# A transformer layer with two attention branches: the forgetting gates are issued behind the first branch, one weight split is held behind the keys, and the row sums of the modulation change places

## The chip, the cores and the metric

The kernel runs on one core of a Trainium2 chip. The metric is device time in microseconds (us) of one execution; lower is better. Three runs of the kernel before the change took 765.37, 765.66 and 765.74 us; the median is 765.66.

## The reference

One decoder layer on 512 positions of width 1024, in float32. Six modulation rows come from a conditioning vector, two attention branches read one projection, and a gated MLP with a short convolution follows.

```python
mod = c @ w_ada + b_ada
sh1, sc1, gt1, sh2, sc2, gt2 = split(mod, 6)
u = x * (1 + sc1) + sh1
q_a, k_a, v_a, f_a, q_b, k_b, v_b, g_a, g_b = split(u @ w_in)
log_f = log_sigmoid(f_a + b_forget)          # 8 heads
cum = cumsum(log_f)
# A, forgetting attention: softmax(q k^T / 8 + cum[t] - cum[s]), s <= t
# B, stick-breaking: A[t,s] = beta[t,s] * prod_{s<j<t}(1 - beta[t,j]),
#    beta = sigmoid(q k^T / 8), s < t
merged = sigmoid(g_a) * (y_fox @ w_fox_proj) + sigmoid(g_b) * (y_sb @ w_sb_proj)
x = layer_norm(alpha * x + (1 + gt1) * (merged @ w_o))
u2 = x * (1 + sc2) + sh2
h_gate, h_val = split(causal_depthwise_conv(u2 @ w_up, width 3))
x = layer_norm(alpha * x + (1 + gt2) * ((silu(h_gate) * h_val) @ w_down))
```

Each branch has 8 heads of 64; the MLP is 2816 wide.

## The kernel before

**Products in three matmuls.** A float32 operand is kept as two tiles of a reduced format: a high part, which ACT makes by a copy (`hi_of`, L99), and a low part, which DVE makes by subtracting the high part from the operand (`lo_of`, L102). A product is three matmuls of 128x128 weights on 512 columns: high by high, high by low, low by high (`mm3`, L131 to L133).

**Items.** Weights come in 128x1024 tiles, *items*, in one list. An item is a DMA on the queue of SyncE (SP) into one of four raw buffers (`LOADS`), and a procedure: the split of weights (`split_proc` and `cut_proc`: high wh, low wl; for the v weights `v_proc`: wvh, wvl; for w_o `wo_proc`: woh, wol), or a *row sum* (`ada_proc`, `mod_col`): modulation values that are first needed after the attention are computed by DVE as a product of a tile of w_ada with the broadcast conditioning row, summed over the columns (L200, 128x1024), and the bias is added (L203). `weights(i, ahead)` issues loads up to item i+3 and runs the procedures up to item i+ahead; a load that needs a raw buffer first runs the procedure that frees it. So an item's place in the list decides when its DVE work is issued, and which loads stand behind it.

**The stream.** The projections (`proj`, `vproj`), branch projections (`bproj`) and the first part of w_o (`o_part`, L714 to L718) are generators in one list, `stream`. `fill(n)` issues n steps of matmuls from it, between the steps of attention, so that PE has work while a head's scores pass through ACT and DVE. `add_pair`, `add_wv`, `add_gate`, `add_ada` and `add_bproj` (L643 to L680) build stream and items together; `add_ada` adds row sums.

**Heads.** The stick-breaking branch (`br` 1) comes first, in pairs of heads, then the forgetting one. For each head `stage_a` makes scores (`scores`, L469 and L470: with s1 and m1, and with s2 and m2, whose last four rows hold the cumulated gates or their counterparts), the sigmoids on ACT (L477: om, one minus beta; L478: pt, beta), and for each of three blocks a reverse running product on DVE (`scan`, L489) and the product with beta (L490). Two one-element memsets on POOL go with it: om's (L486, block 2 only) ahead of the scan, and pt's (L491) behind the product. `stage_b` transposes the weights on PE through the bank set (`turn`, L532) and splits them (ph, pl, and ptc0 and ptc1 for the last blocks). `stage_c` multiplies by v, and adds the two halves into yf on DVE (L567).

**First heads.** Heads 0 and 1 are written out (from L767), with `chain` on: every operation on PE, ACT and DVE is then pinned behind the one issued before it on its engine. In the trace, operations that pass through it have the line of the helper (L68). Elsewhere a scheduler orders the instructions by the code's order and by estimated times. POOL and the DMAs are not pinned.

**Attention tiles.** When the early pool is closed, `open_att` opens a pool in its space: ptc, the s2 and m2 tiles. Memsets on POOL set the rows that hold the gates' counterparts (L325, L328, L330, L331). `fpad`, the padded weights of the forget logits, is one of the tiles in the space that is given up. Its last matmul is in `first_mm(KT - 1, (2, 7))`, group 7; group 2 is the query of pair 1.

**Gates.** `forget_evac` (L336) copies the two halves of the forget logits from their PSUM bank (fq, two copies on ACT), behind the first two heads. `forget` (L340) is issued at head 5: it is pinned behind the last sigmoid of the head before: an add on DVE, then Abs, Exp and Ln on ACT, a DVE operation and the running sum on DVE, and the split into `chi`. `decay_rows` copies the rows of chi by POOL's DMA queue into the s2 and m2 tiles of a forgetting head, once that head's tiles are free.

## Time and profile before

| | |
|---|---|
| median of 3 runs | 765.66 us (765.37 to 765.74) |
| the profiled execution | 764.82 us |
| its span in the trace | 763.0 us |
| granted TensorE clock, mean | 0.995 |
| PE busy | 746.4 us, 98% |
| DVE busy | 550.8 us, 72% |
| ACT busy | 351.9 us, 46% |
| POOL busy | 118.3 us, 16% |
| memory traffic, mean | 129 GB/s |

The engines are PE (matmuls), DVE and ACT (elementwise), POOL and SP, which issues the loads. A row of the timeline gives the start in us from the span's start, the time in us, the engine, line, operation, output and inputs, and in brackets the idle time of the engine ahead of it and what ended that. A row of the waits gives an engine's operation, the one that it waited for, and the total, the count and the longest in us. A row of the windows gives for each engine its busy time with the number of instructions, in the order PE, weight load, DVE, ACT, POOL, SP, and then the granted clock, the DMA share and the rate. Matmuls overlap their neighbours, so their pace is read from their starts. In a row of the DMA issues the last number is the median time from issue to landing.

### The profile page before, as it was taken

What the parts mean: (1) busy time and instruction counts of PE and PEld (TensorE: products, weight loads), DVE (VectorE), ACT (ScalarE), POOL (GpSimd) and SP (SyncE); (2) the same over time, 40 slices, a digit from 0 to 9 for tenths busy, and PEclk for the clock granted to TensorE, in tenths of its full rate; (3) what the DMA queues carried; (4) which work ended last, traced back from release to release, by engine and by line L of the source; (5) the groups of instructions that cost most, each with busy time, mean ns of one, the idle gap of its engine ahead of it and who ended that gap; (6) DMA issues with size and microseconds to landing.
All of it is one profiled execution on the core that took longest, in us unless ns stands there. A gap on an engine that the chain in (4) does not pass through costs nothing.

```text
span 763.0 us, 9469 instructions
## 1 busy us (share of the span) xinstructions
PE 746.4 (98%) x3494; PEld 620.8 (81%) x3494; DVE 550.8 (72%) x893; ACT 351.9 (46%) x586; POOL 118.3 (16%) x130
## 2 busy tenths in 40 slices
PE   8999999899999999999999999999999999999995
PEld 5878788788888888877889888888888888888885
DVE  6977898847787986387897787666666675444866
ACT  3366769537666664242256334444444433122300
POOL 2011000200010000000000950000000134945400
PEclk9999999999999999999999999999999999999998
DMA  8941332313432435545424334343343214423202
GB/s 319 405 161 55 112 111 82 113 37 130 159 119 83 152 128 164 188 141 188 177 62 155 142 126 129 132 139 111 114 134 111 82 56 167 137 84 111 82 34 77
DMA packets 30881, 99.41 MB, mean 130 GB/s; under 512 B 4178, under 2 KB 4690, under 8 KB 30835
## 3 DMA queue, kind: packets, MB, share of 16 engines
q1 hardware_dynamic: 29970, 97.69, 37.7%
q0 software_dynamic: 864, 1.12, 0.5%
q8 instruction: 27, 0.44, 0.3%
q14 instruction: 20, 0.16, 0.1%
HBM read 96.63 MB, written 2.11 MB: 129 GB/s over the span
## 4 chain that ended last, share of the span: by engine, by line
PE 82%; ACT 7%; DVE 6%; DMA 3%; issue 2%; POOL 0%; DVEq 0%; ACTq 0%
PE ps L131 15%; PE ps L132 15%; PE ps L133 15%; PE ps L1006 5%; PE ps L1007 5%; PE ps L1008 5%; PE ps L283 5%; PE ps L560 2%; DMA raw<-in_wa 2%; PE ps L532 2%; ACT wh L99 2%; PE ps L717 1%; PE ps L718 1%; PE ps L716 1%; DVE wl L102 1%
## 5 line engine op out<-in xcount | busy, mean ns | idle before, releaser
L102 DVE TENSOR_TENSOR wl<-raw,wh 128x1024 fp32r<-128x1024 f32 (+2 forms) x101 | 139.9, 1386 | 104.3 <-ACT wh L99 104.0
L99 ACT ACTIVATE wh<-raw 128x1024 fp32r<-128x1024 f32 (+2 forms) x101 | 104.8, 1041 | 112.5 <-PE ps L1008 38.3
L131 PE MATMUL ps<-u2h,wh 128*128 128x512 f32 (+1 forms) x376 | 141.4, 376 | 0.0
L133 PE MATMUL ps<-u2h,wl 128*128 128x512 f32 (+1 forms) x376 | 141.2, 376 | 0.0
L132 PE MATMUL ps<-u2l,wh 128*128 128x512 f32 (+1 forms) x376 | 141.2, 375 | 0.0
L131 PE MATMUL ps<-uh,wh 128*128 128x512 f32 x213 | 84.2, 395 | 1.3 <-ACT fq L68 1.3
L132 PE MATMUL ps<-ul,wh 128*128 128x512 f32 x213 | 83.4, 392 | 0.0
L133 PE MATMUL ps<-uh,wl 128*128 128x512 f32 x213 | 83.1, 390 | 0.0
L131 PEld LDWEIGHTS ps<-u2h,wh 128*128 128x128 f32 x376 | 70.7, 188 | 12.9
L133 PEld LDWEIGHTS ps<-u2h,wl 128*128 128x128 f32 x376 | 70.7, 188 | 12.7
L132 PEld LDWEIGHTS ps<-u2l,wh 128*128 128x128 f32 x376 | 70.7, 188 | 12.7
L627 POOL TENSOR_TENSOR raw<-raw,gt 128x1024 f32<-128x1024 f32 x22 | 60.7, 2766 | 79.2 <-DMA raw<-in_wdn 75.8
L1006 PE MATMUL ps<-wh,hh 128*128 128x512 f32 x128 | 49.8, 389 | 0.0
L1007 PE MATMUL ps<-wl,hh 128*128 128x512 f32 x128 | 49.8, 389 | 0.0
L1008 PE MATMUL ps<-wh,hl 128*128 128x512 f32 x128 | 49.8, 389 | 0.0
L200 DVE SCALAR_TENSOR_TENSOR raw<-raw,cbc 128x1024 f32<-128x1024 f32 x32 | 39.1, 1222 | 14.4 <-DMA raw<-in_wa 14.2
L131 PEld LDWEIGHTS ps<-uh,wh 128*128 128x128 f32 x213 | 40.0, 188 | 9.8 <-ACT fq L68 1.7
L133 PEld LDWEIGHTS ps<-uh,wl 128*128 128x128 f32 x213 | 40.0, 188 | 8.7
L132 PEld LDWEIGHTS ps<-ul,wh 128*128 128x128 f32 x213 | 40.1, 188 | 7.7
L99 ACT ACTIVATE hh<-cv 128x512 fp32r<-128x512 f32 x22 | 13.9, 632 | 61.6 <-DVE cv L986 61.6
L985 ACT ACTIVATE cv<-cv 128x512 f32<-128x512 f32 x22 | 13.9, 632 | 52.3 <-DVE cv L980 52.2
L979 DVE SCALAR_TENSOR_TENSOR cv<-ps,cw,cv 128x511 f32<-128x511 f32 x44 | 32.7, 743 | 2.5 <-ACT cv L978 2.5
(221 smaller groups left out, 1424.3 us busy)
## 6 DMA issues: line engine op xcount, KB each, us to landing
raw<-in_wup SPq DMA_DIRECT2D x44, 512.0 KB, 3.3
raw<-in_wa SPq DMA_DIRECT2D x32, 512.0 KB, 3.3
raw<-in_wct SPq DMA_DIRECT2D x29, 512.0 KB, 3.3
raw<-in_wdn SPq DMA_DIRECT2D x22, 512.0 KB, 3.1
wa<-in_wa SPq DMA_DIRECT2D x14, 512.0 KB, 7.5
raw<-in_wp SPq DMA_DIRECT2D x8, 512.0 KB, 4.1
raw<-in_wo SPq DMA_DIRECT2D x8, 512.0 KB, 3.8
raw<-in_w SPq DMA_DIRECT2D x7, 452.0 KB, 8.1
```

The source lines that it names most:

```text
L99: S.activation(o, i, AF.Copy, scale=scale)
L102: return V.tensor_tensor(o, i, fl(hi), ALU.subtract)
L131: PE.matmul(ps, wh, ah, start=first, stop=False)
L132: PE.matmul(ps, wh, al, start=False, stop=False)
L133: PE.matmul(ps, wl, ah, start=False, stop=last)
L200: V.scalar_tensor_tensor(wt[:, c], wt[:, c], 1.0, cbc[:, c], ALU.mult, ALU.mult, accum_out=raw[:, e : e + 1])
L283: PE.matmul(grp[g], w, u, start=j == 0 and n == 0, stop=j == KT - 1 and n == (1 if g == 7 else 2))
L627: G.tensor_tensor(r, r, gt[1], ALU.mult)
L979: V.scalar_tensor_tensor(t[:, 1:], ps[:, 0:511], cw[:, n, 1:2], t[:, 1:], ALU.mult, ALU.add)
L1006: PE.matmul(ps, hh[j][:, tb], w[0], start=first, stop=False)
L1007: PE.matmul(ps, hh[j][:, tb], w[1], start=False, stop=False)
L1008: PE.matmul(ps, hl[j][:, tb], w[0], start=False, stop=last)
```

## The change

- **The gates.** `forget_evac` is issued right behind `stage_b` of head 0, ahead of the query of pair 1, so under `chain`. `forget` moves from the head of n = 5 to n = 6, ahead of `stage_a` of the first forgetting head, pinned behind head 7's last sigmoid. The rows of all four first forgetting heads are then copied at once, since the stick-breaking heads whose tiles they take have been scored.
- **First heads.** The three matmuls of group 2 for the last k go ahead of the first scores; those on fpad stay behind them.
- **The hold.** For the projections of k, of pairs 2 and later, `proj` first asks for one split less, and issues that one behind the second copy of the pair's second key (`m1`), by `issue_after`.
- **Items.** The 24 row sums stood in the list as 8 with the pairs 5 and 6 (two behind each of q and k), 8 with the gates of the second branch and 8 with its branch projections. Now 3 stand with pair 3, 3 with the last three gates of the first branch, 3 with the queries of pairs 5, 6 and 7, 4 with the first branch's projections, 8 with the second branch's gates as before, and 3 with its branch projections. The v weights come behind q, not k, of a pair, and one more behind pair 3's gates. `vproj` asks for its splits further on by one tile for each block of rows from the third.

```diff
@@ -96,7 +96,7 @@
         return ap.bitcast(F32)
 
     def hi_of(o, i, scale=1.0):
-        S.activation(o, i, AF.Copy, scale=scale)
+        return S.activation(o, i, AF.Copy, scale=scale)
 
     def lo_of(o, i, hi):
         return V.tensor_tensor(o, i, fl(hi), ALU.subtract)
@@ -392,7 +392,7 @@
         r = slice(64 * hh, 64 * hh + 64)
         m1 = z(F32R, "m1")
         hi_of(m1[0:64, :], ps[r, :])
-        hi_of(m1[64:128, :], ps[r, :])
+        state["m"] = hi_of(m1[64:128, :], ps[r, :])
         n = slot_free(idx(br, h))
         m2 = m2z[h] if br == 1 and h < 2 else m2t[n]
         lo_of(m2[0:64, :], ps[r, :], m1[0:64, :])
@@ -436,7 +436,7 @@
 
     def vproj(j, last):
         ps = bank()
-        weights(last, 0)
+        weights(last + max(0, j - 1), 0)
         tb = slice(j * P, (j + 1) * P)
         for k in range(KT):
             h, l = wvs[k]
@@ -449,13 +449,16 @@
 
     ahead = [0]
 
-    def proj(n, after):
+    def proj(n, after, hold=False):
         ps = bank()
-        h, l = weights(n, ahead[0])
+        h, l = weights(n, ahead[0] - hold)
         for k in range(KT):
             mm3(ps, col(h, k), col(l, k), uh[k], ul[k], k == 0, k == KT - 1)
             yield 3
         after(ps)
+        if hold:
+            with tc.issue_after(state["m"].ins):
+                weights(n, ahead[0])
 
     ROWS = ((2,), (3,), (1, 0))
 
@@ -649,9 +652,9 @@
     marks = {}
     seq = PAIRS
 
-    def add_proj(n, after):
+    def add_proj(n, after, hold=False):
         proc = cut_proc if 0 < len(items) <= CUT else split_proc
-        stream.append((proj, (add_item(wct[TILES.index(n)], proc), after)))
+        stream.append((proj, (add_item(wct[TILES.index(n)], proc), after, hold)))
 
     wpi = {}
 
@@ -664,10 +667,11 @@
         br, pr = seq[p]
         for c, ev in (("q", q_evac), ("k", k_evac)):
             if (c, p) in TILES:
-                add_proj((c, p), lambda ps, ev=ev: ev(br, pr, ps))
+                add_proj((c, p), lambda ps, ev=ev: ev(br, pr, ps), p > 1 and c == "k")
                 marks[(p, c)] = len(stream)
-                add_ada({5: 2, 6: 2}.get(p, 0))
-                add_wv(p)
+                if c == "q":
+                    add_ada(p > 4)
+                    add_wv(p)
 
     wvi = []
 
@@ -677,7 +681,7 @@
 
     def add_gate(br, j):
         add_proj(("sb" if br == 1 else "fox", j), gate_after(br, j))
-        add_ada(1 - br)
+        add_ada(br == 0 or j > 4)
 
     gb = list(range(KT))
     for p, ng in ((1, 1), (2, 2), (3, 2), (4, 3)):
@@ -688,6 +692,9 @@
         for _ in range(ng):
             add_gate(1, gb.pop(0))
             add_wv(p)
+        if p == 3:
+            add_wv(p)
+            add_ada(3)
     marks["y1"] = len(stream)
     bj = list(range(KT))
     for p in (5, 6, 7):
@@ -696,6 +703,7 @@
             if bj:
                 j = bj.pop(0)
                 add_bproj(1, j, lambda m, j=j: ma.__setitem__(j, m))
+                add_ada(j % 2)
 
     mh, ml = [], []
 
@@ -732,7 +740,8 @@
     for j in range(3, KT):
         add_gate(0, j)
     for j in range(KT):
-        add_ada()
+        if j % 2 == 0:
+            add_ada()
         add_bproj(0, j, merge(j))
         if j:
             wos.append(add_item(wo[j - 1], wo_proc))
@@ -769,8 +778,9 @@
     for hh in range(2):
         q_half(1, 0, grp[0], hh)
         k_half(1, 0, grp[1], hh)
+    first_mm(KT - 1, (2,))
     scores(1, 0, 2)
-    first_mm(KT - 1, (2, 7))
+    first_mm(KT - 1, (7,))
     st0.close()
     open_att()
     sigmoids(0, 2)
@@ -802,6 +812,7 @@
         turn(1, 0, e)
     process()
     stage_b(1, 0)
+    forget_evac()
     q_half(1, 1, grp[2], 0)
     q_half(1, 1, grp[2], 1)
     fill(24)
@@ -814,21 +825,18 @@
         v_evac(1, j, 0, vf[j])
     process()
     process()
-    forget_evac()
     ahead[0] = AHEAD
     chain["on"] = False
     heads = [(br, 2 * p + e) for br, p in seq for e in range(2)]
-    last = hd[heads[1]]['last']
     for n, (b, h) in enumerate(heads):
-        if n == 5:
-            forget(last)
         f1, f2, f3 = FILL[n // 8]
         if n + 2 < 16:
             if n % 2 == 0:
                 fill_to(marks[(n // 2 + 1, "k")])
                 fill(LEAD)
                 f1 -= LEAD
-            last = hd[heads[n + 1]].get("last")
+            if n == 6:
+                forget(hd[heads[n + 1]]["last"])
             stage_a(*heads[n + 2])
         fill(f1)
         if n + 1 < 16:
```

POOL's queue at the first heads. First before, from the first scan's memset on (om is head 0's block 2, m_n and s_n the m2 and s2 tiles; the words behind a row are the semaphores it waits for):

```order
L486 MEMSET om_571 128x1 [waits Activation_49,Pool_49]
L491 MEMSET pt_572 128x1 [waits Activation_49]
L325 MEMSET m_2_552 4x512 [waits DVE_49,Pool_49]
L325 MEMSET m_3_553 4x512
L325 MEMSET m_0_550 4x512 [waits DVE_49]
L325 MEMSET m_1_551 4x512
L328 MEMSET ptc_542 128x128 [waits DMAHW0_49,PE_49,Pool_49]
L328 MEMSET ptc_543 128x128
L328 MEMSET ptc_544 128x128 [waits DVE_49,PE_49]
L328 MEMSET ptc_545 128x128
```

The same memsets after the change, the rows up to the first scan's:

```order
L328 MEMSET ptc_544 128x128 [waits DVE_49,PE_49,Activation_49]
L328 MEMSET ptc_545 128x128
L330 MEMSET s_0_546 4x512 [waits Pool_49]
L330 MEMSET s_1_547 4x512
L331 MEMSET s_0_546 2x512 [waits Pool_49]
L331 MEMSET s_1_547 2x512 [waits Pool_49]
L330 MEMSET s_2_548 4x512
L330 MEMSET s_3_549 4x512
L331 MEMSET s_2_548 2x512 [waits Pool_49]
L331 MEMSET s_3_549 2x512 [waits Pool_49]
L489 MEMSET om_571 128x1 [waits Activation_49,Pool_49]
L494 MEMSET pt_572 128x1 [waits Activation_49]
```

The two memsets of head 0's scan stood ahead of the twenty of the attention tiles and stand behind them now. (Lines from L460 on are three higher after the change.)

ACT's order around the gates. Before, in the work of heads 4 and 5 (om and pt are sigmoids, m key copies, wvh splits of the v weights, fq the gates):

```order
L477 ACTIVATE om_1225<-ps_1207 128x512
L478 ACTIVATE pt_1226<-ps_1207 128x512
L99 ACTIVATE m_244_1232<-ps_1145 64x512 x2
L343 ACTIVATE fq_498<-fq_499 8x512
L344 ACT_TABLE_LOAD
L344 ACTIVATE fq_498<-fq_498 8x512
L99 ACTIVATE m_245_1236<-ps_1145 64x512 x2
L99 ACTIVATE wvh_1245<-raw_1148 128x512
L99 ACTIVATE ptc_542<-ps_1289 128x384
L99 ACTIVATE wvh_1249<-raw_1148 128x512
L345 ACT_TABLE_LOAD
L345 ACTIVATE fq_498<-fq_498 8x512
```

After, behind head 7's last sigmoids (vv are v's splits, ph the high parts of the turned weights):

```order
L480 ACTIVATE om_1520<-ps_1502 128x512
L481 ACTIVATE pt_1521<-ps_1502 128x512
L99 ACTIVATE vv_1533<-ps_1462 128x2x2x64
L99 ACTIVATE ptc_542<-ps_1570 128x384
L343 ACTIVATE fq_498<-fq_499 8x512
L99 ACTIVATE vv_1536<-ps_1462 128x2x2x64
L99 ACTIVATE ph_1558<-ps_1553 128x512
L344 ACT_TABLE_LOAD
L344 ACTIVATE fq_498<-fq_498 8x512
L99 ACTIVATE ph_1566<-ps_1562 128x384
L345 ACT_TABLE_LOAD
L345 ACTIVATE fq_498<-fq_498 8x512
```

The four operations and their table loads have left the stretch before the turning of head 3's and 4's weights, and stand between the splits behind the stick-breaking branch's end.

DVE's order where the first part of w_o starts. Before (wol low parts of w_o, sg the products of a branch projection, ml merged low parts):

```order
L102 TENSOR_TENSOR ml_3256<-sg_2975,mh_3255 128x512
L200 SCALAR_TENSOR_TENSOR raw_3355,modr<-raw_3355,cbc 128x1024
L102 TENSOR_TENSOR wol_3280<-raw_3190,woh_3278 128x512
L203 TENSOR_TENSOR modc<-modr,bcols 128x1
L102 TENSOR_TENSOR wol_3281<-raw_3190,woh_3279 128x512
L102 TENSOR_TENSOR wol_3298<-raw_3276,woh_3296 128x512
L610 TENSOR_TENSOR sg_3012<-ps_3273,sg_3012 128x512
L102 TENSOR_TENSOR wol_3299<-raw_3276,woh_3297 128x512
```

After:

```order
L102 TENSOR_TENSOR wol_3214<-raw_3202,woh_3212 128x512
L102 TENSOR_TENSOR wol_3215<-raw_3202,woh_3213 128x512
L102 TENSOR_TENSOR wol_3222<-raw_3204,woh_3220 128x512
L102 TENSOR_TENSOR wol_3223<-raw_3204,woh_3221 128x512
L102 TENSOR_TENSOR ml_3243<-sg_2929,mh_3242 128x512
L613 TENSOR_TENSOR sg_2995<-ps_3262,sg_2995 128x512
L712 TENSOR_TENSOR sg_2995<-sg_2995,sg_1306 128x512
```

The row sum (L200, L203) that stood between the wol splits is gone from there.

## Prediction

> **What bounds the kernel now.** I read the page first, then the list of waits, then the timeline around each wait.
>
> ```profile
> PE 746.4 (98%) x3494; PEld 620.8 (81%) x3494; DVE 550.8 (72%) x893; ACT 351.9 (46%) x586; POOL 118.3 (16%) x130
> PE ps L532 <- DVE yf L567: 2.3, 1, 2.3
> PE ps L131 <- ACT fq L68: 1.3, 1, 1.3
> PE ps L717 <- DVE wol L102: 1.0, 2, 0.8
> ```
>
> PE is busy 98% of the 763.0 us, and the change leaves its matmuls as they are. So time can be won only where PE waits, or lost where it is newly made to wait. The three rows after the first are the waits that the change touches. The longest costs more than its 2.3 us, as the timeline of PE shows:
>
> ```profile
> 134.00 0.40 PE L444 MATMUL ps<-wvl,uh 128*128 128x512 f32 x1
> 136.74 0.52 PE L532 MATMUL ps<-idz,pt 128*128 128x128 f32 x3 [2.34 <-DVE yf L567]
> 137.95 0.63 PE L445 MATMUL ps<-wvh,ul 128*128 128x512 f32 x1
> 138.38 0.63 PE L443 MATMUL ps<-wvh,uh 128*128 128x512 f32 x1
> 130.00:140.00 10.00, 7.66 (x35) 6.13 (x35) 8.73 (x14) 8.54 (x16) 4.61 (x11) 0.88 0.52 160
> 77.86 0.50 PE L131 MATMUL ps<-uh,wh 128*128 128x512 f32 x1 [1.28 <-ACT fq L68]
> 78.44 0.40 PE L133 MATMUL ps<-uh,wl 128*128 128x512 f32 x1
> 78.67 0.40 PE L131 MATMUL ps<-uh,wh 128*128 128x512 f32 x1
> ```
>
> A 512-column matmul starts every 0.23 us (78.44, 78.67). After the wait of 2.34 us it is one every 0.43 (137.95, 138.38), and the granted clock of that window is 0.88. From 134.00 to 136.74 PE does one matmul, 2.74 instead of 0.23: 2.5 lost. Of the half pace some 8 matmuls lose 0.2 each, 1.65. The place costs 4.15 us. After the wait of 1.28 at 77.86 the pace is full.
>
> **The first heads, where the change loses.** The POOL rows of the order decide. Before, the one-element memset that head 0's first scan needs goes ahead of the memsets of the attention tiles. In the change it goes behind them, and the third ptc memset waits for the last matmul on fpad, whose space it takes.
>
> ```profile
> 53.25 0.39 PE L68 MATMUL ps<-ul,fpad 128*128 128x512 f32 x1
> 53.14 0.10 POOL L486 MEMSET om<- 128x1 f32 x1 [48.28 <-ACT om L68]
> 55.58 0.64 POOL L328 MEMSET ptc<- 128x128 f32 x4
> 56.28 0.99 POOL L330 MEMSET s<- 4x512 f32 x2
> 59.06 0.98 POOL L331 MEMSET s<- 2x512 f32 x2
> 53.27 0.96 DVE L68 TENSOR_TENSOR_SCAN om<-om,idz 128x383 f32<-128x383 f32 x1 [0.42 <-POOL om L486]
> 57.66 0.69 DVE L68 TENSOR_TENSOR pt<-pt,om 128x511 f32<-128x511 f32 x1
> 60.31 0.95 DVE L68 TENSOR_TENSOR_SCAN om<-om,idz 128x383 f32<-128x383 f32 x1 [0.76 <-POOL pt L491]
> 66.62 1.16 DVE L68 TENSOR_TENSOR pl<-ps,ph 128x512 fp32r<-128x512 f32 x2
> 68.27 0.68 DVE L68 SCALAR_TENSOR_TENSOR s<-ps,s 64x512 fp32r<-64x512 f32 x1
> 75.57 2.36 DVE L68 TENSOR_TENSOR wl<-raw,wh 128x1024 fp32r<-128x1024 f32 x2 [0.44 <-ACT wh L68]
> 77.85 0.67 DVE L342 TENSOR_TENSOR fq<-fq,fq 8x512 f32<-8x512 f32 x1
> 61.35 1.25 PE L68 MATMUL ps<-idz,pt 128*128 128x128 f32 x10
> 67.94 1.25 PE L68 MATMUL ps<-idz,pt 128*128 128x128 f32 x10
> 68.94 0.48 PE L68 MATMUL ps<-uh,wh 128*128 128x512 f32 x1
> ```
>
> The fpad matmul ends at 53.64; with three matmuls put ahead of the first scores, which now wait 0.5 us, it ends about 53.1. Behind it POOL has two ptc memsets (0.35) and eight of s (56.28 to 60.04: 3.76). The om memset comes at 57.2 in place of 53.14, and the scan at 57.3 in place of 53.27: DVE is 4.05 late. At 60.31 DVE had waited 0.76 for POOL, which now is absorbed, less a little overlap: 3.2 late from there.
>
> PE, walked along: the transposes at 61.35 need their last product, which ended at 58.35 and now ends at 62.4, so PE loses 1.1 there and 0.9 is left after what it had gained. The second transposes (67.94, now 68.9) need the banks that the two pl and the ptc empty; these end 3.2 later, at 70.5 to 71.4, and the projection of 68.94 starts at 71.6, 2.7 late. The s remainder of 68.27 comes at 72.1, 3.2 for the lateness and 0.6 for the forget add (0.67 us, from 77.85) which is now ahead of it. From s to the first wl split were 7.3 us of ACT and DVE in turns, so that split starts at 79.4 and ends at 80.6. The matmul that needs it, at 78.44 before, starts at 80.75: **+2.3 us**. The wait on fq of 77.86 is gone, its copies now lie where ACT was idle, but this later wait has swallowed its gain.
>
> The bounds. If POOL did not hold the scan, PE would start that matmul when wl ends, at 76.8 and 0.65 for the forget add, 77.6: -0.85. If DVE kept all of the 4.05, +3.1. I take +2.3, since each step has its row.
>
> **The transposes at 134, where it gains.** The chain that PE waited for:
>
> ```profile
> 120.39 1.28 ACT L344 ACT_TABLE_LOAD   x1
> 130.22 1.28 ACT L599 ACT_TABLE_LOAD   x1
> 117.20 1.79 DVE L489 TENSOR_TENSOR_SCAN om<-om,idz 128x383 f32<-128x383 f32 x2
> L102 DVE TENSOR_TENSOR wvl<-raw,wvh 128x512 fp32r<-128x512 f32 x4 | 2.7, 684 | 0.1
> 135.89 0.69 DVE L567 TENSOR_TENSOR yf<-ps,ytmp 64x512 f32<-64x512 f32 x1
> 110.47 1.22 DVE L102 TENSOR_TENSOR wl<-raw,wh 128x1024 fp32r<-128x1024 f32 x1
> raw<-in_wa SPq DMA_DIRECT2D x32, 512.0 KB, 3.3
> L200 DVE SCALAR_TENSOR_TENSOR raw<-raw,cbc 128x1024 f32<-128x1024 f32 x32 | 39.1, 1222 | 14.4 <-DMA raw<-in_wa 14.2
> ```
>
> The change takes forget's four ACT operations and three table loads of 1.28 (120.39, 130.22 and one between), and its three DVE operations, out of this stretch, and puts three row sums (L200) and two more wvl splits in. The first row sum stands ahead of head 5's scans; its load is issued behind the wl split, which ended at 111.69 and now at 114.2, lands 3.3 later, and the row sum of 1.22 is done at 118.8. The scans start at 118.9 instead of 117.20. From there to yf the order has 3 scans, 3 products, 6 wvl of 0.68, 1 wl and 2 row sums of 1.22, 2 m, 3 turns' remainders, 4 vv and yf itself: 18.0 us by their durations, 1.8 less by overlap, and 1.0 of waiting on ACT, 17.2. yf is done at 136.1, half a microsecond sooner than before (136.58). PE would arrive at its wait at 133.8 without lateness and arrives at 136.1 with it. So the stall nearly goes, 0.15 stays, and the half pace with it: **-4.0 us** of the 4.15. ACT has room, since it loses 3.8 us of table loads there. The bounds: nothing left, -4.15; yf 1.5 later than reckoned, -2.5.
>
> **The o_part steps.**
>
> ```profile
> 341.78 1.23 DVE L200 SCALAR_TENSOR_TENSOR raw<-raw,cbc 128x1024 f32<-128x1024 f32 x1 [1.10 <-DMA raw<-in_wa]
> 343.67 0.50 PE L717 MATMUL ps<-wol,mh 128*128 128x512 f32 x1 [0.77 <-DVE wol L102]
> 355.14 0.50 PE L717 MATMUL ps<-wol,mh 128*128 128x512 f32 x1 [0.24 <-DVE wol L102]
> ```
>
> PE's wol split stood behind a row sum which itself waited 1.10 for its load. In the change no row sum is left there, and the wol splits follow each other. The wait of 0.77 and a restart of 0.16 go, and at 355.14 0.24 and a restart of the same kind: **-1.3 us** (bounds -0.9 and -1.6). The five row sums went ahead, among matmuls for which DVE has time.
>
> **What I cost at nothing.** The gates: they now follow head 7's last sigmoid. That sigmoid waits for scans behind three more row sums, and ends about 154; vv, the Abs, two table loads, Exp, Ln and the DVE sums bring chi to 165.6. The eight row DMAs then go one after the other:
>
> ```profile
> s<-chi POOLq DMA_DIRECT2D x8, 4.0 KB, 3.8
> 175.69 0.80 PE L469 MATMUL ps<-m,s 128*128 128x256 f32 x3 [0.17 <-ACT m L99]
> ```
>
> Issue to landing is 3.8, so the first rows lie ready about 170.5; the scores of 175.69 come at 173.8 or later. Some 3 us cover it, and lateness beyond that costs PE one for one. The hold: by the order it moves whole splits only in pair 2, before matmuls that come 2 us after them, and one wh in pair 6; the waits on m that it is for were 0.17 here. Nothing, with 0.6 to either side. The load order: PE's projections find their splits a tile ahead as before.
>
> **The sum.** The profiled run took 764.82 (span 763.0 and 1.82 around it). +2.3 - 4.0 - 1.3 = -3.0 gives 761.8. The median shown is 0.84 above the profiled run, so 762.7.
>
> **Rivals.** *POOL does not hold the first scan* (its memsets pass earlier): -0.85 at the first heads. PE then reaches the transposes of 134 at 132.9, about 1 us before yf, so 3.2 is won there, and 1.3 later: -5.35, 760.3. Against it stands the order of the queue. 0.13.
>
> *Half pace in the first heads.* In the change PE has, between 68.9 and 71.6, ten transposes (1.0 us) and waits of 1.7. If that counts as idle, the clock halves for the 8 matmuls of before: 1.7 more, 764.4. For it: the 2.34 that halved it had transposes on both sides. Against it: the 1.28 of 77.86 did nothing. 0.15. The Trainium skill, page "TensorE: Matmul & The Clock Gate", section "Why this matters for your kernels", says that only idle gaps above about 3 us halve the clock. The trace has it at 2.34, and the measurement decides. By that page no wait of this change would halve it, and its sum stays the one above. The same page's "Part 4: PE-mode transpose" says that transposes do not count as busy in the same way; by that this rival holds, and the time is its 764.4.
>
> *Slower: DVE carries the whole lateness to head 3's yf.* It is 84% busy there and got three more row sums, each behind a load of 3.3. If yf ends at 139.6 (136.58 and some 3), PE waits 3.5 and the clock halves again: 5.2 in place of 4.15, so +2.3 + 1.0 - 1.3, 767.7. It loses against before from a yf at about 138.9. Against it: between head 2's and head 3's scans DVE waits for ACT at several places, and catches up. 0.08.
>
> *Small waits eat the o_part gain and more* (the hold in pair 6, row sums ahead of m in the second branch): 1.3 to 2, about 764.4. 0.14.
>
> **How the numbers follow.** The forecast has 0.50. A measurement of this kernel tells about 0.2%, 1.5 us, from no change. Faster by more than that (below 764.1): the forecast, the first rival, and half of the second and fourth together less a little, 0.75. Slower (above 767.2): 0.08. Within: 0.17. The range from 760.2 to 764.8 takes in all but the slower rival and the far ends of the others.
>
> **What would show it.** Right: the first scan waits for POOL until about 57.3; PE waits on pt products near 61.5 and on pl or ptc near 70; the matmul of 78.44 at 80.75; no wait above 0.5 us on yf and no granted clock below 1 near 137; no wait on wol near 340. Wrong: the first scan at 53 to 54; a low clock near 71; a wait on yf of over 2 us; a wait on m or s rows at 174.

## The result: slower by 0.8%

| | before | after |
|---|---|---|
| median, 5 runs each | 765.37 us | 770.62 us |
| lowest to highest | 762.53 to 765.74 | 770.25 to 771.37 |
| the profiled execution | 764.82 | 770.58 |
| its span | 763.0 | 768.8 |
| granted TensorE clock, mean | 0.995 | 0.990 |

The ratio is 1.0079, with a 95% interval from 1.0060 to 1.0099. The forecast was 762.7, faster; the range ended at 764.8.

**Where the time went.** PE's order of matmuls is the same but for short stretches in which a few change places, so the start of the matmul with the same number can be compared in the two traces. The last column is what a stretch cost or gave.

| PE's instruction | start before | start after | after is later by | since the row above |
|---|---|---|---|---|
| 163rd | 44.68 | 44.14 | -0.54 | |
| 323rd (first heads done) | 80.29 | 82.27 | +1.98 | +2.52 |
| 563rd | 128.00 | 130.00 | +2.00 | 0.0 |
| 683rd (past the transposes of 134) | 155.67 | 153.56 | -2.11 | -4.11 |
| 763rd | 173.32 | 171.20 | -2.12 | 0.0 |
| 803rd (past the scores of 175) | 181.18 | 182.35 | +1.17 | **+3.29** |
| 923rd | 205.85 | 207.02 | +1.17 | 0.0 |
| 963rd (past the scores of 211) | 214.32 | 221.12 | +6.80 | **+5.63** |
| 1283rd | 277.75 | 285.33 | +7.58 | +0.78 |
| 1763rd (w_o's first part done) | 382.85 | 388.59 | +5.74 | -1.84 |

From there on nothing changes: 5.74 of the 5.8 us between the spans. The 0.54 of the first row was won in the first 12 us, before anything that the forecast treats. The three terms of the forecast are there (2.52, -4.11, -1.84, forecast as 2.3, -4.0, -1.3). What it costed at nothing took 9.7 (3.29, 5.63 and 0.78).

This is the top of the list of PE's waits after the change, without the wait for the first load. The columns are the total, the count and the longest:

```profile
PE ps L472 <- ACT m L99: 5.1, 2, 3.2
PE ps L68 <- DVE pl L68: 1.2, 1, 1.2
PE ps L68 <- DVE pt L68: 1.0, 1, 1.0
PE ps L473 <- DVE m L102: 0.5, 1, 0.5
PE ps L133 <- DVE wl L68: 0.5, 1, 0.5
PE ps L131 <- ACT wh L68: 0.5, 1, 0.5
```

The waits on yf, fq and wol, 4.6 us together, are gone. At the top stands a wait of scores (L472, L469 before) on the copies of the keys, m, which was 0.17 and 0.20 before. The timeline of PE has both places, and two of the first heads:

```profile
62.12 0.98 PE L68 MATMUL ps<-idz,pt 128*128 128x128 f32 x7 [0.96 <-DVE pt L68]
80.30 0.50 PE L133 MATMUL ps<-uh,wl 128*128 128x512 f32 x1 [0.53 <-DVE wl L68]
175.31 0.79 PE L472 MATMUL ps<-m,s 128*128 128x256 f32 x3 [1.91 <-ACT m L99]
215.18 1.33 PE L472 MATMUL ps<-m,s 128*128 128x256 f32 x3 [3.23 <-ACT m L99]
```

The windows of after give, by engine (PE, weight load, DVE, ACT, POOL), the busy time, then the granted clock, for the old stall and the two new ones:

```profile
130.00:140.00 10.00, 10.00 (x53) 8.51 (x52) 9.24 (x14) 8.10 (x14) 0.79 (x4) 1.00 0.72 250
173.00:181.00 8.00, 6.09 (x26) 4.85 (x25) 5.57 (x13) 6.28 (x13) 1.03 (x2) 0.79 0.21 67
212.00:222.00 10.00, 6.82 (x26) 5.90 (x27) 6.76 (x17) 6.84 (x14) 1.03 (x2) 0.66 0.41 143
```

At 134 PE is never idle and the clock stays full. In the other two windows it is at half pace for a part of the time behind the wait.

**The first heads** went as walked through. POOL and DVE of after:

```profile
55.81 0.98 POOL L331 MEMSET s<- 2x512 f32 x2
56.85 0.10 POOL L489 MEMSET om<- 128x1 f32 x1
56.99 0.95 DVE L68 TENSOR_TENSOR_SCAN om<-om,idz 128x383 f32<-128x383 f32 x1 [4.67 <-POOL pt L494]
```

The small memset comes behind the last s memset, and DVE waits 4.67 us for POOL: the scan starts at 56.99 (57.3 was forecast, 53.27 before).

**The second loss** is plain from DVE. Its timeline:

```profile
200.14 1.23 DVE L200 SCALAR_TENSOR_TENSOR raw<-raw,cbc 128x1024 f32<-128x1024 f32 x1 [4.25 <-DMA raw<-in_wa]
204.07 0.69 DVE L570 TENSOR_TENSOR yf<-ps,ytmp 64x512 f32<-64x512 f32 x1
209.70 0.69 DVE L380 SCALAR_TENSOR_TENSOR s<-ps,s 64x512 fp32r<-64x512 f32 x1
```

The load that the row sum wanted, on SP's queue:

```profile
193.17 0.33 SPq L147 DMA_DIRECT2D raw<-in_wa  x1
```

And what the view of the raw tiles gives for it (another load was issued at 186.11, before the copy shown below, and its landing is not in the trace):

```profile
DMA to landing us min/median/max: 6.9/6.9/6.9
```

A row sum waited 4.25 us for a load that took 6.9 in place of 3.3; yf, which stands behind it on DVE, came at 204.07 (199.53 before), the query's remainder at 209.70 (205.45), and the keys after these. POOL shows what was under way:

```profile
186.45 0.95 POOL L583 DMA_DIRECT2D row<-modc  x1 [7.27 <-DVE modc L203]
197.24 0.56 POOL L584 DMA_DIRECT2D gt<-row  x1 [9.84 <-DMA row<-modc]
```

`gt_tile` turns 1024 modulation values into a row: a copy of 1024 pieces of 4 bytes to DRAM, and a broadcast back. It is issued behind the eighth row sum. With the row sums moved ahead, that was at 186.45 instead of 212.20, and the load of 193.17 fell into its 10 us. The rate of all DMA in after, in GB/s from 186 to 201 us in 40 slices, is zero from 190.1 to 196.5, though the load had been issued:

```profile
GB/s 0 0 44 197 273 295 404 147 60 22 12 0 0 0 0 0 0 0 0 0 0 0 0 0 0 0 0 0 55 98 33 109 44 382 404 437 393 437 339 88
```

**The first loss** is a queue. ACT of after around the gates:

```profile
153.73 0.59 ACT L481 ACTIVATE pt<-ps 128x512 f32<-128x512 f32 x1
164.10 0.63 ACT L99 ACTIVATE chi<-fq 8x512 fp32r<-8x512 f32 x1 [0.55 <-DVE fq L347]
166.00 0.66 ACT L99 ACTIVATE vv<-ps 128x256 fp32r<-128x256 f32 x2 [1.00 <-PE ps L133]
167.48 1.05 ACT L99 ACTIVATE wh<-raw 128x1024 fp32r<-128x1024 f32 x1
173.00 1.04 ACT L99 ACTIVATE wh<-raw 128x1024 fp32r<-128x1024 f32 x1
174.07 1.19 ACT L99 ACTIVATE m<-ps 64x512 fp32r<-64x512 f32 x2
```

The last sigmoid (153.73) and chi (164.10) come about when forecast, and the chi rows were there in time. But the v splits, the weight split and the query of pair 4 stand behind chi on ACT and DVE, and the keys behind them. In the kernel before, ACT had stood idle ahead of that weight split, until PE was done with the tile that it overwrites:

```profile
167.85 1.06 ACT L99 ACTIVATE wh<-raw 128x1024 fp32r<-128x1024 f32 x1 [3.96 <-PE ps L132]
```

From this split to the keys the chain on ACT and DVE is the same in both traces, 6.6 us. In the kernel before it starts when PE lets it, and ends 0.17 behind PE, at the scores of 175.69. After the change PE is 2.12 sooner and would let it start at 165.73; but ACT's queue lets it start at 167.48, 1.75 late. PE's wait of 1.91 is this 1.75 and the 0.17.

**The theories.** A: the row copy holds back SP's loads, and the change had moved it ahead of one; its rival, B, is that DVE has too many row sums there. C: forget, behind head 7, makes the keys late; its rival, D, the row sums and splits around. E: POOL's order makes the first heads late; its rival, F, that what is won there is lost again at the keys.

### The profile page after: what moved, and what is told of

The parts are those of the page before. It is cut to its first block, busy times and chain, and to the rows that moved or that the text cites. A ratio compares the mean times of both kernels' runs of the same rounds, so it can differ in the third digit from the quotient of the medians.

```text
span 768.8 us, 9484 instructions
## 1 busy us (share of the span) xinstructions
PE 748.8 (97%) x3494; PEld 622.4 (81%) x3494; DVE 550.9 (72%) x893; ACT 350.4 (46%) x585; POOL 118.5 (15%) x130
## 3 DMA queue, kind: packets, MB, share of 16 engines
HBM read 96.63 MB, written 2.11 MB: 128 GB/s over the span
## 4 chain that ended last, share of the span: by engine, by line
PE 81%; DVE 9%; ACT 4%; DMA 3%; issue 2%; POOL 1%; SPq 0%; DVEq 0%; ACTq 0%
PE ps L131 16%; PE ps L133 16%; PE ps L132 16%; PE ps L283 5%; PE ps L1016 5%; PE ps L1014 5%; PE ps L1015 5%; DMA raw<-in_wa 2%; PE ps L725 2%; PE ps L724 2%; PE ps L726 2%; PE ps L563 2%; PE ps L535 2%; DVE wl L102 1%; PE ps L473 1%
## 5 line engine op out<-in xcount | busy, mean ns | idle before, releaser
L200 DVE SCALAR_TENSOR_TENSOR raw<-raw,cbc 128x1024 f32<-128x1024 f32 x32 | 38.9, 1219 | 16.7 <-DMA raw<-in_wa 16.7
```

Of the source, the lines that this page charges most:

```text
L200: V.scalar_tensor_tensor(wt[:, c], wt[:, c], 1.0, cbc[:, c], ALU.mult, ALU.mult, accum_out=raw[:, e : e + 1])
```

## The experiments

Each time is a median, beside that of the kernel before on the same chip.

**1. The row copy alone moved.** In `ada_proc` the copy for the first gate row is left out (`w > 3` becomes `w == 5`); it goes behind the last rows of chi:

```diff
-            decay_rows(h + 4)
+            dr = decay_rows(h + 4)
+            if h == 3:
+                with tc.issue_after(dr.ins):
+                    gt[0] = gt_tile(4)
```

> The changed kernel, with one thing moved: the copy of the first gate row (1024 numbers of 4 bytes, row<-modc, and its broadcast gt<-row) goes behind the last copy of a forgetting head's rows on POOL, about 231 us, where no load is issued for some 14 us. The order of PE, DVE, ACT and SP stays word for word. Theory A (the row copy in flight from 186.5 to 197.2 held back the load issued at 193.17, and with it DVE's row sum, yf, the s remainders and the scores at 215.18): the row sum of 200.14 no longer waits 4.25 for its load, PE's wait of 3.23 at 215.18 falls below 0.4 and the half pace behind it goes; 5.4 us less, about 765.2. Theory B (DVE has too many row sums ahead of the keys there): the wait stays at 2.5 or more, the time at 769.5 or more.

Measured: 764.42 (before 764.87; ratio 0.9996, 0.9986 to 1.0005). The list of PE's waits, and the window behind the longest:

```profile
PE ps L472 <- ACT m L99: 2.2, 2, 2.0
```

```profile
174.00:182.00 8.00, 5.99 (x35) 5.20 (x35) 5.86 (x14) 6.90 (x14) 1.03 (x2) 1.00 0.22 67
```

The copy was issued at 224.96, and no load between 224.35 and 242.25. The wait near 215 is gone: 0.2 is left of it. Theory A holds and B falls; without this one DMA of 4 KB in its way the change takes the time of the kernel before. The time is 0.8 less than expected; the wait of 2.0 at 176 left the clock at 1.00 here, while 1.91 had halved it in after, which is worth more than that.

**2. The cause put into the kernel before.** One more copy of that form, from `bcols`, which nothing reads:

```diff
+            if h == 1:
+                with tc.issue_after(dr.ins), ...
+                    G.dma_start(row.rearrange("o (k p) -> p (o k)", p=P), bcols[:, 0, :])
```

> The kernel before, with one more row copy of the same form (1024 numbers of 4 bytes from bcols to DRAM, read by nothing) on POOL's queue behind the row copies of 190.69; the order of PE, DVE, ACT and SP stays word for word. Theory A: the load issued at 192.00 lands only when the copy is through, at about 201 instead of 195.1; the row sum of 195.13 comes at 200.5 or later, the keys' scores of 210.98 wait 3 us or more instead of 0.20, with half pace behind: about 770. Rival: the loads do not feel the copy (it moves only 4 KB), and the time is that of before, 765.4.

Measured: 774.12 (before 764.87; ratio 1.0115, 1.0098 to 1.0131). The timelines of POOL, of SP and of DVE:

```profile
191.14 0.96 POOL L500 DMA_DIRECT2D rowx<-bcols  x1
...
191.94 13.92 SPq L147 DMA_DIRECT2D raw<-in_wa  x2
...
204.27 1.23 DVE L200 SCALAR_TENSOR_TENSOR raw<-raw,cbc 128x1024 f32<-128x1024 f32 x1 [9.61 <-DMA raw<-in_wa]
```

The landing of the two loads, of 191.94 and of 205.53, in the view of the raw tiles, and PE's wait in the list:

```profile
DMA to landing us min/median/max: 3.4/7.8/12.3
```

```profile
PE ps L469 <- DVE wl L102: 8.1, 1, 8.1
```

The load issued 0.8 us behind the copy took 12.3 us; the one of 205.53, when the copy was through, took 3.4. PE's 0.20 became 8.1. The direction was right and the size too small by 4 us: a load that is issued at the head of the copy loses nearly all of it (9.0 of 10.1).

**3. The gates back at head 5**, all else as changed:

```diff
-            if n == 6:
-                forget(hd[heads[n + 1]]["last"])
+        if n == 5:
+            forget(last)
```

> The changed kernel with the gates (forget) back at n = 5, behind the last sigmoid of the head before; all else as changed. Theory C (in the change the four ACT operations, two table loads and three DVE operations of forget stand ahead of the last v splits and so ahead of the weight split and the query copies of pair 4; they make the keys late, 1.91 us at 175.31 and half pace behind it): the wait at 175 falls below 0.4 (3.3 us less there), and the wait on yf at the transposes of 134 comes back with 2 us or more and half pace, about 4 us more; about 771.4 in all. Theory D (the wait at 175 comes from the row sums and splits around it): it stays above 1.5, and the time goes to about 774.

Measured: 768.46 (before 764.87; ratio 1.0041, 1.0026 to 1.0056). PE's timeline at the transposes and at the scores of pair 4, and the window behind the first:

```profile
140.77 0.87 PE L535 MATMUL ps<-idz,pt 128*128 128x128 f32 x3 [1.59 <-DVE yf L570]
...
178.20 0.80 PE L472 MATMUL ps<-m,s 128*128 128x256 f32 x3 [0.17 <-ACT m L99]
```

```profile
138.00:146.00 8.00, 5.98 (x23) 4.34 (x23) 7.57 (x12) 7.10 (x15) 2.84 (x9) 0.79 0.90 320
```

The wait at the keys is 0.17 again and the stall on yf is back, 1.59 with half pace. But PE is ready for these scores at 178.03 and not at 173.40, 4.6 us later, while ACT's last v split ends only 1.2 sooner (166.40 and 167.58); ACT again idles 3.96 for PE ahead of the weight split. So the wait went mostly because PE is late, and this run alone does not show how much forget adds to the late keys. It is 3 us faster than expected: PE now comes late enough at 215 that the late load costs 1.6 there and not 3.2, with the clock at 1.00.

**4. The gates alone moved**, in the kernel before (the reverse of the diff above):

> The kernel before with forget alone moved to n = 6, behind head 7's last sigmoid; forget_evac, the hold, the row sums and the first heads as before. Theory C: the wait of 2.34 on yf at 136.74 goes and the half pace with it (4.1 us), and a wait on pair 4's keys of 1 to 2.5 us takes its place at 172 to 175, since the keys waited 0.17 already before and so have no slack for a PE that comes sooner; net 1.5 to 3 below before, 762 to 763.4. Rival: the keys move along with PE and no wait comes at 175: 760.8. If the stall at 134 was not forget's, 764.9 as before.

Measured: 760.76 (before 764.93; ratio 0.9953, 0.9937 to 0.9968), 4.2 us faster. What I expected fell: no wait came at 175. PE's waits, and ACT's timeline:

```profile
PE ps L469 <- ACT m L99: 0.4, 2, 0.2
```

```profile
147.67 0.59 ACT L478 ACTIVATE pt<-ps 128x512 f32<-128x512 f32 x1
...
158.04 0.63 ACT L99 ACTIVATE chi<-fq 8x512 fp32r<-8x512 f32 x1 [0.55 <-DVE fq L347]
...
163.35 1.06 ACT L99 ACTIVATE wh<-raw 128x1024 fp32r<-128x1024 f32 x1 [1.82 <-PE ps L132]
```

Forget takes as long behind the last sigmoid (10.4 us from pt to chi, as in after), but that sigmoid is 6.06 us sooner, while PE is only 2.4 sooner (4.5 ahead of before, not 2.1). The weight split then waits 1.82 for PE, not PE for the queue. So theory C in its plain form is wrong: forget behind head 7 is late only where head 7 is.

**5. The memsets behind head 0's last scan**, all else as changed: the three loops of memsets leave `open_att` and are called behind `scan(0, 1)`.

> The changed kernel with the memsets of the attention tiles issued behind head 0's last scan, so that the two small memsets of the first scan are no longer behind the ptc and s memsets on POOL. Theory E (POOL's order made the first heads late): the first scan starts at about 53.3 instead of 57.3, PE's waits at 62.12, 70.23 and 80.30 go, 2.8 us won by 81 us. Carried to the end, 767.8. Rival F: the work of the gates at 155 to 175 does not move with PE, the wait of 1.91 at 175.31 grows by what was won, and the time stays at 770.6.

Measured: 767.22 (before 764.87; ratio 1.0030, 1.0018 to 1.0042). The timelines of POOL, DVE and PE:

```profile
53.31 0.10 POOL L491 MEMSET om<- 128x1 f32 x1 [16.26 <-ACT om L68]
...
53.45 0.95 DVE L68 TENSOR_TENSOR_SCAN om<-om,idz 128x383 f32<-128x383 f32 x1 [0.51 <-POOL om L491]
...
77.41 0.50 PE L133 MATMUL ps<-uh,wl 128*128 128x512 f32 x1 [0.53 <-DVE wl L68]
```

The scan starts at 53.45, the waits at 62 and 70 are gone, and that matmul comes at 77.41 instead of 80.30. Theory E holds, and its rival F falls: the time that is won is kept.

**6. Both repairs, 1 and 5:**

> The changed kernel with both earlier repairs: the gate row's copy behind the forgetting heads' rows (as in the run in which it alone was moved) and the memsets of the attention tiles behind head 0's last scan. If the two losses are separate, their gains add: 3.5 us won by 81 us as in the run with the memsets alone, less 0.8 at 134 where PE then waits on yf; no wait of 3 or 4 us near 210; so 2.7 below the 764.4 of the row copy's run, 761.7. Rival: the wait on the keys at 173 to 176 grows by what is won ahead of it, and the time stays at 764.4.

Measured: 762.86 (before 764.93; ratio 0.9976, 0.9964 to 0.9988), 1.6 below run 1 where 2.7 was expected. At the keys PE now waits 2.29, 0.28 more, and ACT starts the weight split without a wait for PE. With the first heads on time the keys are still late, so it isn't the lateness of the first heads that makes them so.

**7. The splits pinned behind the keys**, on top of 6:

```diff
-        h, l = weights(n, ahead[0] - hold)
+            with tc.issue_after(state["m"].ins):
+                h, l = weights(n, ahead[0] - hold)
```

> The run before in this call, and in addition the splits of weights that every projection asks for are pinned behind the second key of the pair before (as the change's hold does for one split). In pair 4 two splits (1.05 on ACT and 1.23 on DVE each), which PE needs only some 32 matmuls after the scores, then stand behind the keys. Theory G (the wait of 1.9 on the keys at 175 is the ACT and DVE queue of pair 4: forget's rest, the v splits and these two splits): the keys come 2 us sooner, the wait falls below 0.5, 1.5 us won, up to 3 where the half pace went with it: 760. Rival: the keys are set by forget alone, the wait stays above 1.3, and the pinned splits make new waits on wh or wl: 762 or more.

Measured: 759.80 (before 764.93; ratio 0.9944, 0.9925 to 0.9963), the fastest of all. ACT's timeline at the keys, and the longest of PE's waits in this part:

```profile
170.30 1.20 ACT L99 ACTIVATE m<-ps 64x512 fp32r<-64x512 f32 x2 [1.52 <-PE ps L133]
...
173.47 1.06 ACT L99 ACTIVATE wh<-raw 128x1024 fp32r<-128x1024 f32 x1
```

```profile
PE ps L131 <- ACT wh L99: 1.5, 2, 1.4
```

The keys wait for PE and not PE for them. The price is one new wait on a split, 1.37 at 122.64. Theory G holds: two splits, wanted only some 32 matmuls later, stood ahead of the keys. They stood there before the change too (167.85 and 173.38), so this is a repair and not what the change had made worse. The change's hold was meant for such splits; it reaches only the one that its own projection asks for, while these two are asked for by the projections behind it, and the scheduler had put them ahead.

**8. Without the hold**, all else as changed (`p > 1 and c == "k"` is left out):

> The changed kernel without the hold: every projection asks for its splits as before. Both theories give the hold no part in the two large waits: at 175 the splits that stand ahead of the keys come from the projections behind, which the hold does not reach, and at 215 the load is late. So 1.9 and 3.2 us stay, and the time is 770.6 within 1. If the hold saves what it is for, new waits on keys of 0.5 or more come at pair 2 (95 to 100) and pair 6, and the time is 772 or more; if it costs, 769 or less.

Measured: 769.52 (before 764.93; ratio 1.0072, 1.0053 to 1.0091). The late load stays and costs 5.13. At the keys PE waits 1.07, not 1.91, with a full clock, which I had not expected. Between this and after stands 1.1 us, within a doubtful half pace; whether the hold costs is open. That it gains is not seen.

**9. The early row sums back** at pairs 5 and 6, all else as changed:

```diff
-                if c == "q":
-                    add_ada(p > 4)
-                    add_wv(p)
+                add_ada({5: 2, 6: 2}.get(p, 0))
+                if c == "q":
+                    add_wv(p)
-        add_ada(br == 0 or j > 4)
+        add_ada(br == 0)
-            add_ada(3)
```

> The changed kernel with the early row sums back: the six that stand with pair 3 and the last three gates of the first branch, and the three with the queries of pairs 5 to 7, go to two behind each of q and k of pairs 5 and 6, as before the change; the four with the first branch's projections stay, so that one stands at every second of the second branch's. Gates, hold, first heads as changed. Theory H (the wait of 1.91 at 175.31 comes from the six row sums on DVE ahead of head 7's last sigmoid together with forget behind it, and the wait of 3.23 at 215.18 from the row copy, which the early sums had brought ahead of a load): both waits fall below 0.4; what stays is the first heads' 2.5 more, the 4.1 less at 134 and 1.8 less where w_o's first part starts: 764.9 + 2.5 - 4.1 - 1.8 = 761.5. Rival I (forget behind head 7 and the first heads' lateness suffice for the late keys): the wait at 175 stays above 1.2, 763 or more. The copy may still meet a load at 210 to 222, then 3 us or more stay there.

Measured: 770.36 (before 764.17; ratio 1.0077, 1.0055 to 1.0098). At 175 there is no wait. But ACT's timeline shows both splits behind the keys:

```profile
173.59 1.20 ACT L99 ACTIVATE m<-ps 64x512 fp32r<-64x512 f32 x2 [0.75 <-DVE m L102]
174.82 2.01 ACT L99 ACTIVATE wh<-raw 128x1024 fp32r<-128x1024 f32 x2
```

So the missing wait doesn't tell the row sums from the splits. The start of head 7's last sigmoid does: from 115 us on two row sums stand ahead of it here and six in after, PE's place is the same within 0.3 us, and it starts at 152.02 and not 153.73, 1.71 sooner, nearly the 1.75 that ACT was late in after. And the copy, now at 209.43, met the load of 213.14, which took 12.2 us. PE waits 2.21 on m at 210.83, then 3.11 and 1.03 on pl, and between its 923rd and 1043rd matmul it falls back by 10.2 us against before. Some 6.1 of it lie at the waits on pl and are the copy's, twice what I gave it. The other 4.1 lie at the wait on m: a row sum of 206.99 had waited 2.40 for its load, before the copy was issued, and waits on m stay there in runs 11 and 12 (1.30 and 2.07), where the copy stands later.

**10. The same with the memsets moved:**

> The same, and the memsets of the attention tiles behind head 0's last scan. 3.5 us less than the run above: 758.0, and faster than before by 0.8 to 0.9%. If the time won in the first heads is lost again at the keys or at 134, 760 or more.

Measured: 767.22 (before 764.17; ratio 1.0040, 1.0028 to 1.0053). The first heads give their 3 us; the copy, at 205.44, still meets loads.

**11. The same with the copy pinned** behind chi's last rows (`tc.issue_after(state["rows"].ins)` around `gt_tile`):

> The run with row sums and memsets both moved, and the gate row's copy pinned behind the last forgetting rows on POOL, so at about 222 instead of 205. There the copy was under way when the loads of 209.15 and 213.38 were issued, and PE lost about 6 us between 200 and 240. Theory A: that loss goes to about 1, and the time to 762 of the profile there less 5, about 758.5 to 759 as a median. The copy now runs while the loads of 228 and perhaps 232 are issued; if DVE's row sum or PE's splits need these at once, 2 to 4 us come back, 761 to 763.

Measured: 768.17 (before 765.10; ratio 1.0041, 1.0026 to 1.0056); nothing won. The timelines of POOL, SP and DVE:

```profile
223.13 0.96 POOL L585 DMA_DIRECT2D row<-modc  x1
...
229.99 0.33 SPq L147 DMA_DIRECT2D raw<-in_wa  x1
...
237.64 1.22 DVE L200 SCALAR_TENSOR_TENSOR raw<-raw,cbc 128x1024 f32<-128x1024 f32 x1 [4.27 <-DMA raw<-in_wa]
```

The loss moved along with the copy: run 10's waits on pl at 221 and 223, 2.2 together, are gone, and PE waits 3.50 at the scores of 241.45. The place that was free in run 1 was not free here.

**12. Eight pieces instead of 1024**, on top of 10:

```diff
+            PE.transpose(ps[0:KT, 0:P], modc[:, w, :], ident)
+            V.tensor_copy(sb[0:KT, 0:P], ps[0:KT, 0:P])
+            G.dma_start(row.rearrange("o (k p) -> (o k) p", p=P), sb[0:KT, 0:P])
```

> The run with row sums and memsets moved, with the first gate row written to DRAM in another form: PE transposes the 128x8 values, DVE copies them out of PSUM, and the copy moves 8 pieces of 512 bytes instead of 1024 of 4. By the order it stands at about 225, near where the pinned copy stood (223.13), which held the load of 229.99 back until DVE's row sum started at 237.64, 4.27 late. Theory A in a sharper form (it is the many pieces, 10 us of them, that hold the loads back): the copy is through in 2 to 4 us, as the 4 KB rows of chi are, no row sum near 230 to 240 waits more than 1 us for its load, PE's wait of 3.50 at 241.45 and the half pace behind it go, 5 to 6 us less than the pinned run's 768.2: 762 to 763. Rival (any copy of POOL's queue holds SP's loads): the load stays 4 us late and the time at 766 to 769.

Measured: 761.57 (before 764.40; ratio 0.9957, 0.9945 to 0.9969). POOL's timeline:

```profile
232.37 0.52 POOL L588 DMA_DIRECT2D row<-grow  x1 [8.14 <-DVE grow L587]
234.88 0.56 POOL L592 DMA_DIRECT2D gt<-row  x1 [1.99 <-DMA row<-grow]
```

The same 4 KB were through 2.2 us after they were issued, not 10, and between 210 and 260 PE waits only once, 0.15. The copy stood 7 us later than I had read from the order, so it met the loads at another point than in run 11; that a load behind it would have been free at 229.99 is not shown. That the long copy is gone, and the loss with it, is; the change of place may have a part in it.

## Why the prediction was wrong

- **The first heads**, +2.3: right, 2.52. The memset behind the s memsets, the scan at 57, the waits at 62 and 70 are as walked, and run 5 shows the cause. The matmul that needs wl starts at 80.30 (80.75 forecast), 1.86 later than before, since PE had 0.54 in hand from the first 12 us.
- **The transposes at 134**, -4.0: right, -4.11. Yf was done by 135.3, sooner than reckoned (136.1). Run 4 alone gives the gain.
- **The o_part steps**, -1.3: -1.84, a little under-sized, and outside its bound of -1.6.
- **"What I cost at nothing. The gates"**: this step failed, with 3.29 us. Its times were nearly right: the sigmoid at 154, chi at 165.6 (the DVE half ended at 165.45), PE's scores not before 173.8 (PE was ready at 173.40). But it priced only chi's rows. It did not ask what else stands behind forget on ACT and DVE. The row to ask was ACT's weight split of 167.85: its idle time of 3.96 was all that the queue ahead of it could lose. The change took this and 1.75 more, since the queue ends 3.7 later (167.58 and 163.90) and PE comes 2.1 sooner. "The waits on m that it is for were 0.17 here. Nothing" went by the wrong row: 0.17 says by how much the chain from the split to the keys is longer than PE's work meanwhile, and not what stands ahead of the chain. The rest of the 3.29 is half pace, and that part is luck: behind the wait of 2.01 in run 1 the clock stayed full. Forget behind head 7 is in time by itself, with 1.82 to spare (run 4). The lateness of the first heads is not the cause (run 6). With the early row sums back, head 7's last sigmoid comes 1.71 sooner (run 9), and with the two splits out of the chain the wait goes (run 7). How much each of the row sums adds was not tried.
- **"The load order: PE's projections find their splits a tile ahead as before"**: this failed, with 5.63 us. It looked at splits, and the load that came late was a row sum's. What held it was a DMA on another queue, which moved with the eighth row sum and which the prediction did not count. Runs 1, 2 and 11 show it, and run 12 agrees. A further 0.78 was lost up to the 1283rd matmul, where PE waits 0.55 on m at 274.32; it was not traced.
- **The rivals.** None of the four is what happened. The clock stayed at 1.00 through the first heads. Head 3's yf was in time. "Small waits" named the second branch's keys, but gave 1.3 to 2 us for all of them. Of the prediction's signs of being wrong one came true, a wait on m at 174 (175.31).

## What to carry to other kernels

Where an instruction moves, follow its DMAs by their queue and by their time: a copy in very small pieces is a stretch of 10 us in which other loads starve, and here it cost nothing only where none was issued. A wait of 0.2 says nothing by itself of the slack behind it. Follow its chain back to where it begins: while that is a wait for PE (3.96 before, 1.82 in run 4) the chain moves along with PE, and a gain ahead of it is kept; when the queue ahead grows past that, PE waits for the excess. And a part that gains by itself (here the gates, 0.5%) is worth running by itself before it is judged with its company.

## What the runs showed that was not expected

**A 4 KB copy stops the other queue.** In the kernel before it took 9.8 us. The rate of all DMA in run 2, from 190 to 206 us in 40 slices, stays mostly at 10 to 50 GB/s from 195 to 203 us with a load under way, where 200 to 320 are usual in the kernel before while it loads:

```profile
GB/s 0 0 0 11 11 0 1 10 246 236 92 31 41 10 31 51 20 31 51 31 41 20 41 10 31 20 41 20 10 10 31 31 20 92 21 0 0 0 0 0
```

The copy's queue has 3.7% of the DMA engines' time in that window, so it doesn't show as traffic. The packet records of the traces have the copy as 16 packets of 256 bytes, 64 pieces each, which all start within 1.3 us (after and run 2); the copy lands 7 to 8 us after the last of them has started. In that time after shows no packet of any queue until 196.65, and in run 2 single packets of the load, 4 KB and 0.16 us each at its start, take up to 4.2 us. The Trainium skill, page "DMA: Bandwidth & Descriptors", section "Queues, rings and completion order", says that each DMA engine takes turns between the queues packet by packet, and that a whole packet, of at most 64 pieces, goes first. The 16 packets of 64 pieces agree with that ceiling; but such a packet took at most 0.6 us, so by turns of a packet alone the load would not have been held up for so long, and what the engines do in that time the traces do not show. The load that meets the copy lands 3.2 us (after) and 3.1 us (run 2) behind the landing of the copy.

**Half pace is not set by the length of the wait.** The granted clock fell behind waits of 1.59 (run 3, 0.79), 1.91 (after, 0.79) and 2.34 (before, 0.79 from 134 to 142), and stayed at 1.00 behind 2.01 (run 1) and 2.29 (run 6, 172 to 180). In the clock records of the traces it lasts 3.41 us each time, or 6.83 (after, from 214.08), and where one trace has it twice the two begins lie a whole number of 3.41 us apart: 37.55 in after, 11 of them, and 78.50 in run 2, 23. So the clock seems to change at fixed marks, and whether a wait of some 2 us is caught would depend on where it falls between them; that is inferred, no run moved a wait against the marks. The 1.65 us that went with the stall of 134 is then a chance and not a rule, and it goes with a part of the spread of one kernel's runs: the kernel before ran in 762.27 us with a mean clock of 0.997, and in 765.40 with 0.994. The Trainium skill, page "TensorE: Matmul & The Clock Gate", section "Why this matters for your kernels", puts the limit at idle gaps of about 3 us; here 1.59 was enough, and the measurement decides.
